# A ring of two raw weight places instead of four, earlier expert weights, first projection weights ahead of the other transfers

## The chip, the cores and the metric

The kernel runs on one core of a Trainium2 chip. The metric is device time in microseconds (us) of one execution. Three runs of the kernel before gave 681.19 us as the median (680.13 to 682.99). The profile shown here is of one execution that took 680.27 us, of which the profiler's span holds 678.3.

## The reference

One layer on 256 tokens of width 1024, in float32: a norm, one wide projection, a mixer of two branches (a sparse attention with compressed, selected and windowed keys, and a gated recurrence, HGRN2), a gated merge with two branch projections, an output projection with residual, and then a mixture of 32 experts, two per token, and a last norm. What matters for the time is cut to this:

```python
def reference(x, ...):
    h = rmsnorm(x, attn_norm)
    proj = h @ w_in                                   # 1024 x 4888
    o_nsa = nsa_mixer(...); o_hg = hgrn2_mixer(...)
    mixed = gate_nsa * (o_nsa @ w_br_nsa) + gate_hg * (o_hg @ w_br_hg)
    x = x + mixed @ w_out
    x = x + hier_moe(rmsnorm(x, ffn_norm), ...)
    return rmsnorm(x, final_norm)

def hier_moe(h, ...):
    ...
    for e in range(32):                               # w_gate, w_up 1024 x 512, w_down 512 x 1024
        hid = silu(t @ w_gate[e]) * (t @ w_up[e])
        out = out + combine[:, e:e + 1] * (hid @ w_down[e])
```

## The kernel before, in words

The work has two stages. **The front** computes everything up to the router. Its weights come as 30 blocks of 1 MB (two of them smaller) in the order of the list `FRONT`: f0, f1, q0, q1, c0, c1, b0, b1, a0, a1, i0, i1, g0, g1, m20 to m31, h0, h1, m00 to m11, n0, n1, o00, o10, o01, o11. A block is loaded into a *raw* place (`load_front`), then split into a high and a low part (`split_part`): ScalarE copies the high part in a reduced format, VectorE subtracts it from the raw block. TensorE then forms three products per pair (`three`: all high products first, L442, then high by low and low by high, L444 and L445). The split of a block is issued when the block before it begins on TensorE, and `load_front` is called behind it. A split is also held back until the third last group of products so far has ended (`HOLD`, `marks`). Attention and recurrence steps stand in the list `todo` and are put between groups of products (`fill`).

**The experts** follow in eight rounds of four (`hidden`, `prepare`, `down`): gate product, up product, down product. Their weights are 96 matrices of 2 MB, loaded by `load_expert` in the order of the list `pieces`: in the first round four gate pieces (`k`), four up, then down pieces, one of them in halves.

**Memory.** All large tiles with the tag `w2` share 11 double slots of 2 MB (16 KB of each partition): the input, the raw ring, the parts of each block (`wsp`), long-lived data of the front, and the expert pieces. A second tag `w` has three slots of 1 MB. Which slot a tile gets is decided when the program is built: one whose earlier tile is no longer needed. Nearly all transfers stand in one queue, SyncE's (SP): each is issued in order, and a transfer that waits for its place holds up all behind it. The table `EARLY` names front blocks at which expert pieces are put into that queue, so that experts' weights come while the front still computes. In each engine's own queue the order is fixed when the program is built, too, by a scheduler that works with its own estimates.

The first round's expert weights are 13 pieces. After them, the next transfer (the second round's gate weights) needs a place that the first round's gate product frees.

Of the kernel before, what the change touches and what calls it, by code (L numbers as in the profile page):

```python
# [9 lines left out]
F32 = mybir.dt.float32  # L10
# [58 lines left out]
def _level_masks():  # L69
# [4 lines left out]
    while h < 128:  # L74
# [10 lines left out]
FRONT = ["f0", "f1", "q0", "q1", "c0", "c1", "b0", "b1", "a0", "a1", "i0", "i1", "g0", "g1",  # L85
         "m20", "m21", "m30", "m31", "h0", "h1", "m00", "m01", "m10", "m11",
         "n0", "n1", "o00", "o10", "o01", "o11"]
WIDTH = {n: 2048 for n in FRONT}
WIDTH["c0"] = WIDTH["c1"] = 1120
FOFF = {}  # L90
# [82 lines left out]
CUTS = [slice(0, 256), slice(256, 512)]  # L173
LAST = [(slice(0, 2), slice(0, 1024)), (slice(2, 4), slice(0, 512)), (slice(2, 4), slice(512, 768)), (slice(2, 4), slice(768, 1024))]
GATE_V = (0, 0)
EARLY = {"a0": 1, "i1": 1, "m31": 1, "m10": 1, "n0": 1, "o00": 1, "o10": 1, "o01": 2}
HOLD = 3
FILLS = {"n0": 2, "m10": 3, "m20": 1, "m11": 3, "m01": 3, "m00": 3, "h0": 1, "h1": 1, "i": 1, "m30": 1, "g": 1}

# [2 lines left out]
def tile_block(ctx, tc, x, xp, xa, xb, wf, wcmp, vec, rows, consts, lmask, w_gate, w_up, w_down, out, dbg=None, manual=False):  # L182
    nc = tc.nc
    PE, V, S, G = nc.tensor, nc.vector, nc.scalar, nc.gpsimd
    dbg = dbg or {}

    cp = ctx.enter_context(tc.tile_pool(name="cp", bufs=1))
# [9 lines left out]
    def pair(name, dtype=F32):  # L197

        return big.tile([128, 4096], dtype, tag="w2", bufs=PAIRS, name=name)
# [17 lines left out]
    def two(t, n=1024, **k):  # L217
        return t[:, :n], t[:, n:]
# [6 lines left out]
    def load_x(name, src):  # L225
        t = slot(name)
        v = t.rearrange("p (t d) -> p t d", t=2)
        for tt in range(2):
            nc.sync.dma_start(v[:, tt], src[128 * tt:128 * tt + 128, :])
        return v  # L230

    xs = two(pair("xab"), 2048)
# [4 lines left out]
    vc_ = cp.tile([128, vec.shape[1]], F32, name="vc_")  # L237
    kept = _C["causal"][0]
    cs = cp.tile([128, kept], F32, name="cs")
    cm_ = kb2("2x", "cm_")  # L240
    lm = cp.tile([128, 8, 128], U8, name="lm")

    def row(name, t):
        o, n = ROWS[name]
        nc.sync.dma_start(t, bass.AP(tensor=rows.tensor, offset=rows.offset + o, ap=[[0, 128], [1, n]]))
        return t
# [8 lines left out]

    ident = C("ident")
    raws, his, los, marks, splits = {}, {}, {}, [], []
    ring = [h for _ in range(2) for h in two(pair("raw"), 2048)]
    to_load, to_split = list(FRONT), list(FRONT)

    def load_front():
        if to_load:
            n = to_load.pop(0)
            w = WIDTH[n]
            raws[n] = ring[FRONT.index(n) % 4][:, :w]
            step = w // 2 if n == FRONT[0] else w
            for o in range(0, w, step):
                nc.sync.dma_start(raws[n][:, o:o + step], bass.AP(tensor=wf.tensor, offset=wf.offset + FOFF[n] + 128 * o,
                                                                  ap=[[step, 128], [1, step]]))
                if n == FRONT[0] and o == 0:  # L270
                    nc.sync.dma_start(xs[1][:, :1024], xb)

    def after(i):

        return tc.issue_after(getattr(i, "ins", i))

    def split_part(n, c, behind=()):

# [74 lines left out]

    load_front()
    load_front()
    nc.sync.dma_start(vc_, vec)
    nc.sync.dma_start(cs, consts[:, :kept])
    xv = load_x("x", x)
    load_front()
    nc.sync.dma_start(cm_[:, :consts.shape[1] - kept], consts[:, kept:])  # L360
    hgn = row("hgn", cm_[:, 384:])
    brow = row("br", cp.tile([128, 36], F32, name="brow"))
    lmf = slot("lmf")[:, :1152].rearrange("p (l t) -> p l t", l=9)
    nc.sync.dma_start(lmf, lmask)


    hh_, hl_ = two(pair("hhl", F32R), 2048)
# [53 lines left out]
    def token_factors():  # L421

        prx = bank("ns", "prx")
        with after(marks[-3]):
            PE.matmul(prx[:, :256], one.to_broadcast([128, 128]), rxd, start=True, stop=True)
        V.tensor_copy(rxb, prx[:, :256])

    rt = VC("rt").rearrange("p (k e) -> p k e", k=8)
    G.memset(ones, 1.0)
# [2 lines left out]
        G.tensor_copy(before, lmf[:, 8])  # L432
        G.tensor_tensor(rt, rt, VC("fe")[:, :, None].to_broadcast([128, 8, 36]), op=OP.mult)
    wcm = slot("wcm")
    nc.sync.dma_start(wcm, wcmp)
    dump("hT", hhi.bitcast(F32))


# [578 lines left out]
    xv = load_x("x2", xp)  # L1017
# [455 lines left out]
```

## Time and profile before

| | before |
|---|---|
| median of 3 runs | 681.19 us |
| the profiled execution | 680.27 us |
| its span | 678.3 us |
| TensorE (PE) busy | 548.6 us, 81% of the span |
| VectorE (DVE), ScalarE (ACT) busy | 212.8 us, 145.4 us |
| transfers | 238.84 MB, mean 352 GB/s |
| experts' weights in the chain that ended last | 20% up, 15% gate, 16% down |

The page's slices show two stages. Up to about 240 us TensorE is busy all the time and the transfers come and go; after that the transfers run at about 427 GB/s to the end, and TensorE is busy in parts. Time that an engine idles while another is the bound costs nothing.

### The profile page before, as it was taken

The numbers are of one execution on the slowest core, as the hardware profiler recorded it, in microseconds if no ns is written. First come the engines' busy times: TensorE is split into PE (matmuls) and PEld (weight loads), VectorE is DVE, ScalarE is ACT, GpSimd is POOL, SyncE is SP. The second block draws the span as 40 slices with busy tenths as digits, with TensorE's granted clock in tenths as the row PEclk, the third lists the DMA queues.
The fourth block names the chain that finished last, engine by engine and source line by source line (L and its number), as shares of the span: only waits on it lengthen the run. The fifth ranks groups of instructions, "written<-read, shape, count | busy, mean of one in ns | idle before, by whom it ended". The sixth has DMA issues, their size and how long they took to land.

```text
span 678.3 us, 8658 instructions
## 1 busy us (share of the span) xinstructions
PE 548.6 (81%) x3692; PEld 314.8 (46%) x3692; DVE 212.8 (31%) x430; ACT 145.4 (21%) x235; POOL 32.0 (5%) x50
## 2 busy tenths in 40 slices
PE   8989999999999999987758468766846877594574
PEld 6988777888898854342114114212411421141121
DVE  5686856777558342121002102101210110020012
ACT  5433348466455310100000000000000000000003
POOL 0411500200000000000000000000000000000001
PEclk8999999999999999989679788967968796697888
DMA  8856463463578999999999999999999999999993
GB/s 343 346 190 229 143 254 119 151 230 129 191 269 320 425 421 427 427 422 431 427 428 427 426 426 426 429 425 432 423 426 431 422 429 428 426 427 429 420 389 119
DMA packets 26443, 238.84 MB, mean 352 GB/s; under 512 B 2720, under 2 KB 5280, under 8 KB 10144
## 3 DMA queue, kind: packets, MB, share of 16 engines
q1 hardware_dynamic: 26112, 237.44, 84.9%
q8 instruction: 31, 0.51, 0.3%
q10 hardware_dynamic: 288, 0.79, 0.3%
q14 instruction: 12, 0.10, 0.0%
HBM read 237.17 MB, written 1.05 MB: 351 GB/s over the span
## 4 chain that ended last, share of the span: by engine, by line
DMA 50%; PE 29%; DVE 1%; ACT 0%; issue 0%; SPq 0%; POOL 0%; POOLq 0%; DVEq 0%; ACTq 0%
DMA we<-in_w_up 20%; DMA we<-in_w_gate 15%; DMA wh<-in_w_down 10%; DMA wd<-in_w_down 6%; PE pu L1258 5%; PE pws L442 3%; PE pws L445 3%; PE pws L444 3%; PE pg L1258 2%; PE py L1315 2%; PE pga L1146 2%; PE pwo L442 1%; PE pwo L445 1%; PE pwo L444 1%; PE pno L903 1%; PE pnt L880 1%
## 5 line engine op out<-in xcount | busy, mean ns | idle before, releaser
L1258 PE MATMUL pg<-we,xe 128*32 128x512 f32 x512 | 94.3, 723 | 52.1 <-DMA we<-in_w_gate 52.1
L1258 PE MATMUL pu<-we,xe 128*32 128x512 f32 x512 | 91.2, 721 | 47.3 <-DMA we<-in_w_up 43.5
L1286 DVE SCALAR_TENSOR_TENSOR h<-pu,wv,h 128x512 f32<-128x512 f32 x8 | 8.7, 1089 | 246.2 <-PE pu L1258 246.2
L286 DVE TENSOR_TENSOR wsp<-raw,wsp 128x2048 fp32r<-128x2048 f32 (+3 forms) x34 | 68.2, 2011 | 33.7 <-ACT wsp L282 33.5
L1258 PEld LDWEIGHTS pg<-we,xe 128*32 128x32 f32 x512 | 20.1, 128 | 121.7 <-DMA we<-in_w_gate 73.4
L1258 PEld LDWEIGHTS pu<-we,xe 128*32 128x32 f32 x512 | 20.4, 129 | 113.1 <-DMA we<-in_w_up 61.9
L282 ACT ACTIVATE wsp<-raw 128x2048 fp32r<-128x2048 f32 (+3 forms) x34 | 56.3, 1663 | 45.0 <-PE pws L445 14.9
L1298 ACT ACTIVATE ys<-py,wv 128x512 fp32r<-128x512 f32 (+1 forms) x17 | 11.3, 663 | 243.2 <-PE py L1315 211.8
L1315 PE MATMUL py<-wh,hT 128*32 128x512 f32 x112 | 49.4, 594 | 3.7 <-DMA wh<-in_w_down 3.7
L1315 PE MATMUL py<-wd,hT 128*32 128x512 f32 x336 | 50.6, 595 | 0.0
L445 PE MATMUL pws<-hhl,wsp 128*128 128x256 f32 x192 | 49.3, 288 | 0.7 <-DVE wsp L286 0.7
L444 PE MATMUL pws<-hhl,wsp 128*128 128x256 f32 x192 | 49.1, 287 | 0.0
L1280 ACT ACTIVATE h<-pg,wv 128x512 f32<-128x512 f32 x8 | 9.2, 1144 | 150.6 <-PE pg L1258 150.6
L445 PEld LDWEIGHTS pws<-hhl,wsp 128*128 128x128 f32 x192 | 37.4, 195 | 1.0 <-DVE wsp L286 0.9
L444 PEld LDWEIGHTS pws<-hhl,wsp 128*128 128x128 f32 x192 | 37.4, 195 | 0.0
L442 PE MATMUL pws<-hhl,wsp 128*128 128x256 f32 x192 | 34.1, 297 | 1.3 <-ACT hhl L401 1.3
L1299 DVE SCALAR_TENSOR_TENSOR ys<-py,wv,ys 128x512 fp32r<-128x512 f32 (+1 forms) x17 | 12.2, 719 | 69.0 <-ACT ys L1298 68.4
L1146 PE MATMUL pga<-lm,x 128*128 128x128 f32 x256 | 30.3, 276 | 0.0
L444 PE MATMUL pxs<-wsp,hhl 128*128 128x512 f32 (+1 forms) x80 | 29.9, 377 | 0.2 <-DVE wsp L286 0.2
L442 PEld LDWEIGHTS pws<-hhl,wsp 128*128 128x128 f32 x192 | 27.3, 194 | 5.1 <-ACT hhl L401 2.4
L445 PE MATMUL pxs<-wsp,hhl 128*128 128x512 f32 (+1 forms) x80 | 29.5, 372 | 0.0
L1146 PEld LDWEIGHTS pga<-lm,x 128*128 128x128 f32 x256 | 29.3, 192 | 0.2 <-DVE lm L1137 0.2
(252 smaller groups left out, 684.3 us busy)
## 6 DMA issues: line engine op xcount, KB each, us to landing
we<-in_w_gate SPq DMA_DIRECT2D x32, 2048.0 KB, 34.3
we<-in_w_up SPq DMA_DIRECT2D x32, 2048.0 KB, 34.5
wd<-in_w_down SPq DMA_DIRECT2D x21, 2048.0 KB, 39.1
raw<-in_wf SPq DMA_DIRECT2D x27, 1024.0 KB, 4.8
wh<-in_w_down SPq DMA_DIRECT2D x15, 1024.0 KB, 30.0
wd<-in_w_down SPq DMA_DIRECT2D x3, 1024.0 KB, 35.6
wd<-in_w_down SPq DMA_DIRECT2D x3, 512.0 KB, 23.6
wd<-in_w_down SPq DMA_DIRECT2D x6, 256.0 KB, 8.6
```

The lines of the kernel that those rows point to most:

```text
L282: i = S.activation(his[n][:, c], raws[n][:, c], AF.Copy)
L286: splits.append((i, V.tensor_tensor(los[n][:, c], raws[n][:, c], his[n][:, c].bitcast(F32), op=OP.subtract)))
L442: PE.matmul(out_, lh, rh, start=start and i == 0, stop=False, skip_group_check=True)
L444: PE.matmul(out_, lh, rl, start=False, stop=False, skip_group_check=True)
L445: last = PE.matmul(out_, ll, rh, start=False, stop=stop and i == n - 1, skip_group_check=True)
L1146: i = PE.matmul(pgs[q, n][:, 128 * k:128 * k + 128], xv[:, tt, 512 * n + 128 * k:512 * n + 128 * k + 128], sel[q][:, tt], start=tt == 0 an ...
L1258: i = PE.matmul(p[32 * e:32 * e + 32], xes[q][:, k, 32 * e:32 * e + 32], W["k", k // 2][:, e, k % 2] if by_rows else W[4 * q + e][:, k], s ...
L1280: S.activation(h, pg.rearrange("p (c j) -> p c j", j=4), AF.Silu, scale=r)
L1286: V.scalar_tensor_tensor(h, pu.rearrange("p (c j) -> p c j", j=4), r, h, op0=OP.mult, op1=OP.mult)
L1298: return (S.activation(hi[:, c], p[:, c], AF.Copy, scale=wv), V.scalar_tensor_tensor(lo[:, c], p[:, c], wv, hi[:, c].bitcast(F32), op0=OP. ...
L1299: V.scalar_tensor_tensor(lo[:, c], p[:, c], wv, hi[:, c].bitcast(F32), op0=OP.mult, op1=OP.subtract))
L1315: PE.matmul(py[n][32 * e:32 * e + 32], hTs[q][:, j, 32 * e:32 * e + 32], WD[4 * q + e, j][:, 512 * n:512 * n + 512], start=j == 0, stop=j ...
```

## The change

- The raw ring has two places of 1 MB in one double slot (it had four in two). The first three loads become two, and a block's load waits for the split of the block two before it instead of four. One double slot more is left for parts (`wsp`) and expert pieces.
- `EARLY` puts eleven expert pieces into the queue during the front instead of nine: new ones at b0, a second at n0 and one at n1; the one at i1 is gone.
- The first half of f0 is issued ahead of the second half of the input (`xb`); vectors, constants and the input for the norm follow f1, the masks and `wcmp` follow whatever block was last issued.
- The copy of the token factors (`rxb`) is put behind the last split.

```diff
-EARLY = {"a0": 1, "i1": 1, "m31": 1, "m10": 1, "n0": 1, "o00": 1, "o10": 1, "o01": 2}
+EARLY = {"b0": 1, "a0": 1, "m31": 1, "m10": 1, "n0": 2, "n1": 1, "o00": 1, "o10": 1, "o01": 2}
...
-    ring = [h for _ in range(2) for h in two(pair("raw"), 2048)]
+    ring = two(pair("raw"), 2048)
+    last_dma = []
...
-            raws[n] = ring[FRONT.index(n) % 4][:, :w]
+            raws[n] = ring[FRONT.index(n) % 2][:, :w]
...
-                nc.sync.dma_start(raws[n][:, o:o + step], bass.AP(tensor=wf.tensor, offset=wf.offset + FOFF[n] + 128 * o,
-                                                                  ap=[[step, 128], [1, step]]))
+                i = nc.sync.dma_start(raws[n][:, o:o + step], bass.AP(tensor=wf.tensor, offset=wf.offset + FOFF[n] + 128 * o,
+                                                                      ap=[[step, 128], [1, step]]))
+                last_dma.append(i)
                 if n == FRONT[0] and o == 0:
-                    nc.sync.dma_start(xs[1][:, :1024], xb)
+                    with after(i):
+                        nc.sync.dma_start(xs[1][:, :1024], xb)
...
     load_front()
     load_front()
-    nc.sync.dma_start(vc_, vec)
-    nc.sync.dma_start(cs, consts[:, :kept])
-    xv = load_x("x", x)
-    load_front()
-    nc.sync.dma_start(cm_[:, :consts.shape[1] - kept], consts[:, kept:])
-    hgn = row("hgn", cm_[:, 384:])
-    brow = row("br", cp.tile([128, 36], F32, name="brow"))
+    with after(last_dma[-1]):
+        nc.sync.dma_start(vc_, vec)
+        nc.sync.dma_start(cs, consts[:, :kept])
+        xv = load_x("x", x)
     lmf = slot("lmf")[:, :1152].rearrange("p (l t) -> p l t", l=9)
-    nc.sync.dma_start(lmf, lmask)
+    with after(last_dma[-1]):
+        nc.sync.dma_start(cm_[:, :consts.shape[1] - kept], consts[:, kept:])
+        hgn = row("hgn", cm_[:, 384:])
+        brow = row("br", cp.tile([128, 36], F32, name="brow"))
+        nc.sync.dma_start(lmf, lmask)
...
-        V.tensor_copy(rxb, prx[:, :256])
+        with after(splits[-1][1]):
+            V.tensor_copy(rxb, prx[:, :256])
...
-    nc.sync.dma_start(wcm, wcmp)
+    with after(last_dma[-1]):
+        nc.sync.dma_start(wcm, wcmp)
```

Three places show what the built programs make of it. The first is the head of SP's queue. Before (the third row holds the two halves of f0, the next f1; the first `raw_74` is q0, the second q1):

```order
L271 DMA xab_67<-in_xb 128x1024
L268 DMA raw_73<-in_wf 128x1024 x2
L268 DMA raw_73<-in_wf 128x2048
L356 DMA vc__69<-in_vec 128x328
L357 DMA cs_70<-in_consts 128x202
L229 DMA x_81<-in_x 128x1024
L229 DMA x_81<-in_x 128x1024 [waits DMAHW0_49]
L268 DMA raw_74<-in_wf 128x2048 [waits DMAHW1_49]
L360 DMA cm__71<-in_consts 128x384 [waits DMAHW2_49]
L245 DMA cm__71<-in_rows 128x128 [waits DMAHW3_49]
L245 DMA brow_87<-in_rows 128x36 [waits DMAHW4_49]
L364 DMA lmf_89<-in_lmask 128x1152 [waits DMAHW5_49]
```

Now, from f1 on (the last two rows are q0 and q1):

```order
L273 DMA raw_73<-in_wf 128x2048
L360 DMA vc__69<-in_vec 128x328
L361 DMA cs_70<-in_consts 128x202
L229 DMA x_80<-in_x 128x1024
L229 DMA x_80<-in_x 128x1024 [waits DMAHW0_49]
L365 DMA cm__71<-in_consts 128x384 [waits DMAHW1_49]
L245 DMA cm__71<-in_rows 128x128 [waits DMAHW2_49]
L245 DMA brow_86<-in_rows 128x36 [waits DMAHW3_49]
L368 DMA lmf_83<-in_lmask 128x1152 [waits DMAHW4_49]
L273 DMA raw_73<-in_wf 128x2048 [waits DMAHW5_49,DVE_49]
L273 DMA raw_73<-in_wf 128x2048 [waits DMAHW6_49,DVE_49]
```

q0 has moved from before the constants and masks to behind them, and it now waits for VectorE's split of f0.

The second place is SP's queue at the end of the front. Before (the raw rows are o10, o01 and o11; the `we` rows the last gate piece and the four up pieces):

```order
L321 DMA we_1750<-in_w_gate 128x4x1024 [waits PE_49,Pool_49]
L268 DMA raw_74<-in_wf 128x2048 [waits DMAHW6_49,DVE_49]
L268 DMA raw_73<-in_wf 128x2048 [waits DMAHW7_49,DMAHW4_49,DVE_49]
L326 DMA we_1861<-in_w_up 128x4096 [waits PE_49]
L268 DMA raw_73<-in_wf 128x2048 [waits DMAHW0_49,DVE_49]
L326 DMA we_1996<-in_w_up 128x4096 [waits PE_49]
L229 DMA x2_1985<-in_xp 128x1024 [waits Pool_49]
L229 DMA x2_1985<-in_xp 128x1024 [waits DMAHW1_49]
L326 DMA we_2025<-in_w_up 128x4096 [waits DMAHW2_49,DVE_49,PE_49]
L326 DMA we_2059<-in_w_up 128x4096 [waits DMAHW3_49,DVE_49,PE_49]
L331 DMA wd_2061<-in_w_down 128x4096 [waits DMAHW6_49,DMAHW4_49,DVE_49]
```

Now (the raw rows are o00, o10, o01 and o11):

```order
L273 DMA raw_73<-in_wf 128x2048 [waits DMAHW7_49,DMAHW2_49,DVE_49]
L329 DMA we_1859<-in_w_up 128x4096 [waits PE_49]
L273 DMA raw_73<-in_wf 128x2048 [waits DMAHW1_49,DVE_49]
L329 DMA we_1861<-in_w_up 128x4096 [waits PE_49]
L273 DMA raw_73<-in_wf 128x2048 [waits DMAHW2_49,DVE_49]
L329 DMA we_1926<-in_w_up 128x4096 [waits PE_49]
L229 DMA x2_1987<-in_xp 128x1024 [waits DMAHW0_49,PE_49,Pool_49]
L229 DMA x2_1987<-in_xp 128x1024
L273 DMA raw_73<-in_wf 128x2048 [waits DMAHW4_49,DVE_49]
L329 DMA we_1999<-in_w_up 128x4096 [waits DMAHW3_49]
L334 DMA wd_2028<-in_w_down 128x4096 [waits PE_49]
```

The up pieces have moved ahead by a place or more, and o01 and o11 stand behind two and three of them, each behind a wait for VectorE.

The third place is ScalarE's queue at the end of the front: the high parts of o00, o10, o01, o11 (`wsp`), the merged branch (`mT`), the residual's squares (`sqs`). Before:

```order
L282 ACTIVATE wsp_1922<-raw_74 128x2048 [waits DMAHW1_49,PE_49,Activation_49]
L1019 ACT_TABLE_LOAD
L1019 ACTIVATE warm_97<-mhalf_96 128x1
L999 ACTIVATE mT_1890<-mg_1123 128x512 [waits DVE_49,Activation_49]
L999 ACTIVATE mT_1890<-mg_1123 128x512 [waits DVE_49]
L282 ACTIVATE wsp_1993<-raw_74 128x2048 [waits DMAHW3_49,PE_49]
L999 ACTIVATE mT_1953<-mg_1123 128x512 [waits DVE_49] x2
L282 ACTIVATE wsp_2022<-raw_73 128x2048 [waits DMAHW4_49,DVE_49,PE_49]
L282 ACTIVATE wsp_2056<-raw_73 128x2048 [waits DMAHW6_49,DVE_49,PE_49]
L1043 ACTIVATE sqs_2051,st_94<-x2_1985 128x512 [waits DMAHW0_49,DVE_49]
```

Now:

```order
L1025 ACT_TABLE_LOAD
L1025 ACTIVATE warm_95<-mhalf_94 128x1
L1005 ACTIVATE mT_1890<-mg_1121 128x512 [waits DVE_49,Activation_49]
L1005 ACTIVATE mT_1890<-mg_1121 128x512 [waits DVE_49]
L285 ACTIVATE wsp_1922<-raw_73 128x2048 [waits DMAHW2_49,PE_49]
L1005 ACTIVATE mT_1955<-mg_1121 128x512 [waits DVE_49] x2
L285 ACTIVATE wsp_1995<-raw_73 128x2048 [waits DMAHW4_49,PE_49]
L285 ACTIVATE wsp_2025<-raw_73 128x2048 [waits DMAHW6_49,PE_49,Activation_49]
L1049 ACTIVATE sqs_2054,st_92<-x2_1987 128x512 [waits DMAHW0_49,DVE_49]
L285 ACTIVATE wsp_2059<-raw_73 128x2048 [waits DMAHW2_49,PE_49,Activation_49]
```

Each of these splits has moved behind work that it stood ahead of: o00 and o10 behind a pair of `mT` rows, o11 behind the first square. In the built program the parts of o11 now lie in the slot that held the parts of o01; before they lay in one that a gate of the merge had left.

## Rows read from the trace of the kernel before

**Rows 1.** The page: its first line, and transfers in 40 slices.
```profile
span 678.3 us, 8658 instructions
...
DMA  8856463463578999999999999999999999999993
GB/s 343 346 190 229 143 254 119 151 230 129 191 269 320 425 421 427 427 422 431 427 428 427 426 426 426 429 425 432 423 426 431 422 429 428 426 427 429 420 389 119
```

**Rows 2.** Chain that ended last, in time: start, us, what; from 209 us.
```profile
209.59 0.47 PE pwo L442 x2
...
225.94 0.45 PE pwo L442 x2
...
227.31 0.88 PE pxt L1057 x8
...
234.56 0.81 PE prt L1067 x8
...
243.86 7.00 PE pg L1258 x64
...
260.68 29.07 DMA we<-in_w_up
```

**Rows 3.** SP's timeline: start, us, engine, line, operation; 234.8 to 246.5 us.
```profile
234.97 0.43 SPq L339 DMA_DIRECT2D wh<-in_w_down  x1
...
245.77 0.33 SPq L326 DMA_DIRECT2D we<-in_w_gate  x1
```

**Rows 4.** The tile wh's transfer issued at 234.97 us, from issue to landing.
```profile
DMA to landing us min/median/max: 15.6/15.6/15.6
```

**Rows 5.** The tile we's transfer issued at 245.77 us, from issue to landing.
```profile
DMA to landing us min/median/max: 9.7/9.7/9.7
```

**Rows 6.** The tile we's transfer issued at 209.62 us, from issue to landing.
```profile
DMA to landing us min/median/max: 7.9/7.9/7.9
```

**Rows 7.** Busy time by engine from 205 to 210 us; last: clock, DMA share, GB/s.
```profile
205.00:210.00 5.00, 5.00 (x42) 4.91 (x41) 5.00 (x7) 3.34 (x5) 0.00 (x0) 1.00 0.44 182
```

**Rows 8.** The page, transfers by line: count, KB each, us to landing.
```profile
raw<-in_wf SPq DMA_DIRECT2D x27, 1024.0 KB, 4.8
```

**Rows 9.** ScalarE's timeline, 199 to 220 us; in brackets the idle time before.
```profile
206.75 1.92 ACT L282 ACTIVATE wsp<-raw 128x2048 fp32r<-128x2048 f32 x1 [0.32 <-PE pws L445]
211.00 1.23 ACT L999 ACTIVATE mT<-mg 128x512 fp32r<-128x512 f32 x2 [2.33 <-DVE mg L997]
...
217.81 1.92 ACT L282 ACTIVATE wsp<-raw 128x2048 fp32r<-128x2048 f32 x1 [2.05 <-PE pwo L445]
```

**Rows 10.** VectorE's timeline, 200 to 222 us.
```profile
203.87 0.69 DVE L995 TENSOR_TENSOR mg<-pws,mg 128x512 f32<-128x512 f32 x1 [1.12 <-PE pws L445]
...
219.76 2.29 DVE L286 TENSOR_TENSOR wsp<-raw,wsp 128x2048 fp32r<-128x2048 f32 x1 [1.67 <-ACT wsp L282]
```

**Rows 11.** ScalarE's timeline at the start: the high part of q0.
```profile
16.76 1.92 ACT L282 ACTIVATE wsp<-raw 128x2048 fp32r<-128x2048 f32 x1 [1.34 <-DMA raw<-in_wf]
```

**Rows 12.** GpSimd's timeline at the start: the first use of the masks.
```profile
21.49 1.04 POOL L431 CAST lm<-lmf 128x1024 uint8<-128x1024 f32 x1 [3.35 <-DMA lmf<-in_lmask]
```

**Rows 13.** TensorE's timeline at the start: first instructions of product groups.
```profile
10.80 1.28 PE L442 MATMUL pws<-hhl,wsp 128*128 128x256 f32 x4
...
13.59 0.67 PE L442 MATMUL pws<-hhl,wsp 128*128 128x256 f32 x4
...
22.50 0.82 PE L442 MATMUL pws<-hhl,wsp 128*128 128x256 f32 x4
...
26.99 0.64 PE L442 MATMUL pws<-hhl,wsp 128*128 128x256 f32 x4
...
28.43 0.64 PE L442 MATMUL pws<-hhl,wsp 128*128 128x256 f32 x4
```

**Rows 14.** TensorE's waits, 26 to 60 us: line, releaser, us in total, times, longest.
```profile
PE phl L574 <- DVE hg L564: 1.4, 1, 1.4
PE pws L445 <- DVE wsp L286: 0.7, 1, 0.7
```

More of the change, by code (lines that the diff above doesn't have):

```diff
@@ L257, in tile_block, with after @@
     raws, his, los, marks, splits = {}, {}, {}, [], []
-    ring = [h for _ in range(2) for h in two(pair("raw"), 2048)]
+    ring = two(pair("raw"), 2048)
+    last_dma = []
     to_load, to_split = list(FRONT), list(FRONT)
+    def after(i):
+        return tc.issue_after(getattr(i, "ins", i))
     def load_front():
@@ L264, in load_front @@
             w = WIDTH[n]
-            raws[n] = ring[FRONT.index(n) % 4][:, :w]
+            raws[n] = ring[FRONT.index(n) % 2][:, :w]
             step = w // 2 if n == FRONT[0] else w
             for o in range(0, w, step):
-                nc.sync.dma_start(raws[n][:, o:o + step], bass.AP(tensor=wf.tensor, offset=wf.offset + FOFF[n] + 128 * o,
-                                                                  ap=[[step, 128], [1, step]]))
+                i = nc.sync.dma_start(raws[n][:, o:o + step], bass.AP(tensor=wf.tensor, offset=wf.offset + FOFF[n] + 128 * o,
+                                                                      ap=[[step, 128], [1, step]]))
+                last_dma.append(i)
                 if n == FRONT[0] and o == 0:
-                    nc.sync.dma_start(xs[1][:, :1024], xb)
-    def after(i):
-        return tc.issue_after(getattr(i, "ins", i))
+                    with after(i):
+                        nc.sync.dma_start(xs[1][:, :1024], xb)
     def split_part(n, c, behind=()):
```

## Prediction

> **What bounds the kernel now.** I read the page's slices of the transfers first [rows 1]: they run at about 427 GB/s from slice 13 (220 us) to the end, and below that in nearly every slice before. So there are two regimes, and the question is how one hands over to the other. The chain that ended last, read in order of time [rows 2], shows it: TensorE's products up to 250.86 us (the first round's gate product begins at 243.86), and from about 260 us on transfers of expert weights, the first of them a wait of 29.07 us. The front is bound by TensorE, the rest by the transfers, which never pause again. The end is therefore fixed by one event, the landing of the first transfer of the second round; all behind it follows at the same pace, whatever the change does. In SP's timeline this transfer is issued at 245.77 us [rows 3], when the gate product has freed its first place, and it lands 9.7 us later, at 255.5 [rows 5]. It lands behind the last piece of the first round, issued at 234.97 and landed 15.6 us later, at 250.6 [rows 3, 4]. So in the kernel before the queue is not yet empty when the first place comes free. 4.9 us lie between the two landings, which is 2 MB at 427 GB/s [rows 1]. A 2 MB transfer that finds the queue nearly empty takes 7.9 us from issue to landing [rows 6], 3.0 more than its own 4.9.
>
> This gives the rule for the sum. With D as the delay of TensorE at its first gate product, the first transfer of the second round is issued at 245.8 + D and lands at the later of two times: 245.8 + D + 7.9, or 4.9 after the last piece of the first round. The end shifts by as much as this landing differs from 255.5. Even with D = 0 the best is 253.7, a gain of 1.8 us: 2 MB less in the queue would save 4.9, but 3.0 to 3.1 of that are lost because the queue runs dry before a place is free.
>
> The Trainium skill, "DMA: Bandwidth & Descriptors", section "Anatomy of one DMA", gives a fixed part of about 2.0 us (measured on GpSimd's path) and 436 GB/s for the rest; by it 2 MB would take an estimated 6.8 us where the row has 7.9, and the sum below would come out 1.1 us lower. The row decides.
>
> **The change part by part.**
>
> *An expert piece more, early.* The piece at b0 goes into a stretch in which the transfers have room (107 to 254 GB/s in slices 4 and 5 [rows 1]). It costs nothing there, and takes 2 MB, 4.9 us, from the backlog. By the rule above it is worth 1.8 us at most.
>
> *The end of the front, on ScalarE and VectorE.* Here the loss lies. In the built order the split of o10 has gone behind the second pair of merged rows on ScalarE, the split of o11 behind the first square, and the parts of o11 lie in the slot of those of o01. TensorE's blocks take 5.45 us each: o00 begins at 209.59, o11 three blocks later at 225.94 [rows 2]. A high part takes 1.92 us on ScalarE [rows 9], a low part 2.29 on VectorE, an evacuation 0.69 [rows 10].
> - o00: its low part comes behind the evacuation of n1's first half and ends at about 210.6, one us into the block; the four high products that now stand first (4 x 0.23 us, from 0.45 for two [rows 2]) cover 0.9. Cost 0.1.
> - o10: its high part ran at 206.75, ahead of the second pair of `mT`, which ran at 211.00 [rows 9]. Now it follows that pair. The pair's second half needs n1's last products (209.6); VectorE takes it up when o00's low part and a merged row are done (211.2), spends two operations of 0.65 (212.5), ScalarE copies 0.6 (213.1), then o10's high part to 215.0 and its low part to 217.3. TensorE is there at 215.1, has 0.9 of high products, and waits from 216.0 to 217.4: 1.35.
> - o01: its raw block is issued when o00's low part is done, 210.6, and lands 4.8 us later [rows 8], at 215.4; parts by 219.7, needed at 221.9. Cost nothing.
> - o11: its high part ran at 217.81 [rows 9] and its low part at 219.76 [rows 10], well ahead of 225.94. Now the high part cannot begin until TensorE has left o01, at 225.94 + 1.45 = 227.4. It is done at 229.3, the low part at 231.6. Meanwhile TensorE has eight transposes (0.88 us in [rows 2]), which wait 0.3 for the residual's second add, then idles 0.8 until 229.35, does four high products, waits 0.35 for ScalarE's copies, and has the logits until the low part is there. Cost 1.45.
> Together 0.1 + 1.35 + 1.45 = 2.9 us, all on TensorE's path to the gate product. Behind the ring's waits are queued, on SP, the up pieces, the second copy of x and o11 itself: from 205 to 210 us the transfers were busy for 0.44 of the time before [rows 7]; now a gap of some 2 us comes at 211, and I count the last piece of the first round to land near 250 (14 MB from 215.4, 2.45 us each). So 4.9 after it is 255, and the first of the two times decides.
>
> *The start.* The first half of f0 ahead of `xb` lets TensorE begin up to 1.1 us earlier. But q0 pays for it: it has gone behind x, the constants, the rows and the masks. Before it landed by 16.76 [rows 11], the masks at 21.49 [rows 12]; the sum of bytes up to both is the same, so q0 now lands at about 21.4. Its high part is done at 23.35, its low part at 25.65. TensorE wants the low part after four high products: it began q0 at 22.50 and q1 at 28.43 [rows 13], so it is 2.5 us late, and what f0 won in front of this wait is gone. Of these 2.5 the stall of 0.7 in q1 goes (its low part is now in time), and 1.4 are a stall that TensorE has at the first diagonal product anyway [rows 14]: VectorE, which it waits for there, is busy with its own queue and, as I count it, gets to that point no later. 0.4 is left. Bounds: 0 (another 0.6 in such stalls is to be had further on), and 2.5 + 1.4 = 3.9 if nothing is absorbed and the first groups after the wait run at half clock (below). I take 0.4, as the stall's row stands right there.
>
> *The ring of two.* A block's load now starts when the split two blocks before it is done. One block is four groups of 1.44 us (26.99 to 28.43 [rows 13]), 5.8, and more with fills; a load takes 4.8 [rows 8] and a split 4.2. Two blocks are 11.5, so 2.5 us remain, and the splits are held back by TensorE's marks in any case. Cost 0; behind an expert piece, at 9.7 [rows 5], it would be up to 2.4 late. *The fourth slot for parts*: ScalarE's splits wait for TensorE's products of the held-back group [rows 9], as far as the row tells, not for a slot; worth 0. *The copy of the token factors* stood behind the same split before: 0.
>
> **The sum.** D = 2.9 + 0.4 = 3.3. First transfer of the second round: 245.8 + 3.3 + 7.9 = 257.0, against 255.5: the end comes 1.5 us later. The profiled execution took 680.27 us, its span 678.3 and 2.0 around it, which gives 681.8. It lay 0.9 below the median of 681.19, so the forecast is 682.7. About 0.5% (3.4 us) is what a measurement of this kernel can tell from no change; the forecast lies inside it, 681 to 684.5 as its own range.
>
> **The rivals.**
> 1. *The earlier piece pays in full.* If the waits of o10 and o11 are covered and TensorE reaches its gate product 3.1 us earlier than before, 4.9 are saved: 676.3. For it speaks that the queue is the bound from there on; against it that D would have to be -3.1, while the order of the queues gives 2.9 on the other side. Between D = -1.6 and 5.2 it ends as no change. Chance 0.08 of over 0.5%.
> 2. *The clock falls in the new waits.* TensorE begins its work at the start after an idle gap, and soon after it the groups from 10.80 take 2.8 us (to 13.59) where a later one takes 1.44 [rows 13]: the granted clock is at half, 1.2 instead of 2.4 GHz, for some 3.2 us, which costs about 1.6. If this follows the wait in q0 and the one at o11, and nothing of the first is absorbed, D is 3.3 + 3.2, the first transfer lands at 260.2, and the end is 4.7 late: 685.9. It decides from D = 5.2 on. For it: two waits of over one us in short succession. Against it: the stall of 1.4 at the first diagonal [rows 14] is followed by no such stretch. The Trainium skill, "TensorE: Matmul & The Clock Gate", section "HAM oscillation — how this bites in real kernels", says that waits for data between bursts of products throttle the clock again; this is that rival. Chance 0.22.
> 3. *The ring of two starves TensorE in mid-front.* Four expert pieces ahead of raw blocks at up to 2.4 us each: D up to 13, 689 or more. Against it: a raw load is issued ahead of each piece, and the next comes a block later. Chance 0.04.
>
> **How the numbers follow.** Forecast 0.66, rivals 0.08, 0.22 and 0.04. Faster by over 0.5%: 0.08; within 0.5%: 0.66; slower: 0.26. The range of 8 in 10 leaves out rival 1 in full and the far end of rivals 2 and 3: 678.5 to 687.
>
> **What would show it.** Right: the gate product begins 2.5 to 4.5 us later; the first transfer of the second round takes about 8 us, not 9.7; ScalarE's last raw split begins when o01's products end; q0's high part begins at 21 to 23; the diagonal's stall is gone. Wrong: a gate product no later than 243.9, a split of o11 ready when TensorE comes to it, q0 in time, or half-clock stretches before 250.

## The result, and the profile after

The changed kernel takes 687.18 us (median of 6 runs, 684.62 to 688.22), the kernel before, run beside it, 680.13 (6 runs). The ratio is 1.0098 [1.0084, 1.0112]: slower by 1.0%, more than the 0.5% that I called no change. The forecast was 682.7, 1.5 later than the kernel before; measured are 7.05, and the time lies just outside the range (687.0). Of the cases on record, rival 2 came in the main, the clock that falls in the new waits (685.9, chance 0.22), and not the likeliest.

The page's lines for the changed kernel, which answer to [rows 1]:

```profile
span 685.3 us, 8659 instructions
...
DMA  8648533363479989999999999999999999999993
GB/s 319 244 158 311 208 124 123 124 246 123 176 312 372 417 351 428 430 427 425 428 428 425 428 427 427 428 426 428 425 427 428 424 430 428 428 425 428 421 394 122
```

The two regimes are still there: about 427 GB/s from slice 15 on (257 us; counted from 0, as the prediction counts), less before. In the kernel before that began with slice 13. What has moved is the place of the handover. SP's timeline (start, us, engine, line, operation) at the issue of the last piece of the first round and of the first of the second, which answers to [rows 3]:

```profile
243.48 0.42 SPq L342 DMA_DIRECT2D wh<-in_w_down  x1
254.28 2.04 SPq L329 DMA_DIRECT2D we<-in_w_gate  x2
```

and from issue to landing of the transfer at 254.28, where [rows 5] had 9.7:

```profile
DMA to landing us min/median/max: 7.8/7.8/7.8
```

It lands at 262.07, 6.6 us later than in the kernel before. The last piece of the first round, issued at 243.48, took this long:

```profile
DMA to landing us min/median/max: 11.2/11.2/11.2
```

So it had landed at 254.67, 7.4 earlier: the first transfer of the second round finds a queue that is all but empty and takes what [rows 6] said it would. TensorE's timeline has the gate product in the changed kernel and in the kernel before at

```profile
252.29 1.06 PE L1264 MATMUL pg<-we,xe 128*32 128x512 f32 x8
...
243.79 0.64 PE L1258 MATMUL pg<-we,xe 128*32 128x512 f32 x4
```

So D is 8.5, where my sum had 3.3.

TensorE's timeline of the changed kernel where q0 begins (in brackets the idle time before and what ended it), against [rows 13]:

```profile
23.04 0.74 PE L448 MATMUL pws<-hhl,wsp 128*128 128x256 f32 x4 [2.63 <-ACT wsp L285]
...
25.37 0.58 PE L451 MATMUL pws<-hhl,wsp 128*128 128x256 f32 x1 [1.47 <-DVE wsp L289]
...
27.02 1.05 PE L448 MATMUL pws<-hhl,wsp 128*128 128x256 f32 x4
...
29.59 0.63 PE L448 MATMUL pws<-hhl,wsp 128*128 128x256 f32 x2
```

Two waits, with five products between them; behind them a group takes 2.57 us (27.02 to 29.59), where one takes 1.44 in [rows 13]. (q0's block, asked for at 11.96, had landed 9.0 us later, at 20.99.) The table by stretches says why. Its last three columns are the granted clock, the transfers' share and GB/s; first the changed kernel, then the kernel before, in the same two stretches:

```profile
24.40:31.20 6.80, 5.83 (x27) 5.83 (x28) 5.72 (x8) 3.06 (x4) 0.61 (x1) 0.50 0.52 175
...
236.00:240.00 4.00, 4.00 (x13) 3.24 (x13) 0.00 (x0) 0.00 (x0) 0.00 (x0) 0.57 0.98 408
```
```profile
24.40:31.20 6.80, 6.14 (x51) 5.94 (x51) 3.70 (x5) 3.60 (x4) 1.21 (x1) 1.00 0.82 322
236.00:240.00 4.00, 3.69 (x47) 3.51 (x48) 3.55 (x19) 1.15 (x4) 0.80 (x2) 1.00 1.00 428
```

The clock is at its lower level, 1.2 GHz, from 24.39 to 31.21 us, with 27 products where the kernel before has 51; and once more from 236.01 to 239.43. The last four blocks wait where the prediction put the waits:

```profile
214.14 0.50 PE L450 MATMUL pwo<-wsp,mT 128*128 128x512 f32 x1 [0.27 <-DVE wsp L289]
220.87 0.50 PE L450 MATMUL pwo<-wsp,mT 128*128 128x512 f32 x1 [0.98 <-DVE wsp L289]
231.96 0.66 PE L1063 MATMUL pxt<-cs,x 128*128 128x128 f32 x4 [0.34 <-DVE x L1041]
233.23 1.18 PE L448 MATMUL pwo<-wsp,mT 128*128 128x512 f32 x4 [0.61 <-ACT wsp L285]
```

The shift against the kernel before, block by block: f0 -1.5, f1 -2.4, q0 +0.5, q1 +4.75, c0 +3.8, then +3.34 to +3.38 from b0 to o00, o10 +3.9, o01 +5.2, o11 +7.5, gate product +8.5. Between c0 and b0 there are two moves: behind the first diagonal product, where TensorE waits less than before, the shift is down to +2.1, and at b0 it goes up again by 1.3. There TensorE waits for VectorE, which is late with b0's low part:

```profile
50.90 1.97 PE L606 MATMUL phl<-hg,hg 128*128 128x64 f32 x16 [1.05 <-DVE hg L623]
```

In the kernel before this wait is 0.48. b0's raw block was asked for at 37.89, when the split of c0 had freed its place in the ring of two, and took

```profile
DMA to landing us min/median/max: 6.2/6.2/6.2
```

where the same block in e2 and e4 (below) takes 4.6 and 4.7 and costs nothing. No transfer stood ahead of it in the queue. So there are three losses, 2.1 at the start, 1.3 at b0 and 5.2 at the end of the front; the second is rival 3 in small, though without the weight piece ahead of the block that rival 3 supposed.

### The profile page after: what moved, and what is told of

Read it like the earlier page. It is cut to its first block, busy times and chain, and to the rows that moved or that the text cites. A ratio compares the mean times of both kernels' runs of the same rounds, so it can differ in the third digit from the quotient of the medians.

```text
span 685.3 us, 8659 instructions
## 1 busy us (share of the span) xinstructions
PE 554.9 (81%) x3692; PEld 317.4 (46%) x3692; DVE 213.6 (31%) x430; ACT 145.3 (21%) x235; POOL 33.5 (5%) x50
## 3 DMA queue, kind: packets, MB, share of 16 engines
HBM read 237.17 MB, written 1.05 MB: 348 GB/s over the span
## 5 line engine op out<-in xcount | busy, mean ns | idle before, releaser
L285 ACT ACTIVATE wsp<-raw 128x2048 fp32r<-128x2048 f32 (+3 forms) x34 | 56.2, 1663 | 48.7 <-PE pws L451 21.4
L1321 PE MATMUL py<-wd,hT 128*32 128x512 f32 x336 | 53.6, 609 | 0.0
L1321 PE MATMUL py<-wh,hT 128*32 128x512 f32 x112 | 50.8, 608 | 3.5 <-DMA wh<-in_w_down 3.5
L451 PE MATMUL pws<-hhl,wsp 128*128 128x256 f32 x192 | 50.0, 291 | 1.5 <-DVE wsp L289 1.5
L450 PE MATMUL pws<-hhl,wsp 128*128 128x256 f32 x192 | 49.7, 289 | 0.0
L451 PEld LDWEIGHTS pws<-hhl,wsp 128*128 128x128 f32 x192 | 38.1, 198 | 1.8 <-DVE wsp L289 1.7
L450 PEld LDWEIGHTS pws<-hhl,wsp 128*128 128x128 f32 x192 | 38.1, 198 | 0.0
L448 PE MATMUL pws<-hhl,wsp 128*128 128x256 f32 x192 | 34.8, 299 | 3.9 <-ACT wsp L285 2.6
L448 PEld LDWEIGHTS pws<-hhl,wsp 128*128 128x128 f32 x192 | 27.6, 197 | 8.2 <-ACT wsp L285 3.0
```

Source lines behind the costliest of these rows:

```text
L285: i = S.activation(his[n][:, c], raws[n][:, c], AF.Copy)
L448: PE.matmul(out_, lh, rh, start=start and i == 0, stop=False, skip_group_check=True)
L450: PE.matmul(out_, lh, rl, start=False, stop=False, skip_group_check=True)
L451: last = PE.matmul(out_, ll, rh, start=False, stop=stop and i == n - 1, skip_group_check=True)
L1321: PE.matmul(py[n][32 * e:32 * e + 32], hTs[q][:, j, 32 * e:32 * e + 32], WD[4 * q + e, j][:, 512 * n:512 * n + 512], start=j == 0, stop=j ...
```

## The experiments

Twelve runs followed: eleven kernels, and the changed one again. *D* is the start of the first gate product against the 243.79 of the kernel before, *landing* that of the first gate piece of the second round, both in the profiled execution; the ratio is to the kernel before on the same chip (there its median lies between 679.5 and 680.1, so compare ratios rather than medians).

| run | D | landing | span | median | ratio |
|---|---|---|---|---|---|
| before | 0 | 255.5 | 678.3 | 680.1 | |
| changed | +8.5 | 262.1 | 685.3 | 687.2 | 1.0098 [1.0084, 1.0112] |
| e1 q0 ahead | +0.2 | 256.2 | 679.0 | 679.1 | 0.9989 [0.9977, 1.0002] |
| e2 old pieces | +2.7 | 258.6 | 681.4 | 684.5 | 1.0072 [1.0049, 1.0096] |
| e3 both | -3.3 | 252.2 | 676.3 | 677.7 | 0.9968 [0.9955, 0.9981] |
| e4 clock held | +2.9 | 257.0 | 680.7 | 683.3 | 1.0056 [1.0038, 1.0074] |
| e5 tenth piece | -3.2 | 252.2 | 675.1 | 676.7 | 0.9952 [0.9940, 0.9965] |
| e6 without n1 | -3.1 | 253.3 | 676.2 | 678.1 | 0.9979 [0.9969, 0.9988] |
| e7 pieces alone | +2.7 | 256.6 | 680.3 | 681.6 | 1.0028 [1.0017, 1.0039] |
| e8 f0 second | -1.4 | 253.9 | 678.3 | 680.0 | 0.9994 [0.9984, 1.0004] |
| e9 f0 first | -0.8 | 254.7 | 677.8 | 679.6 | 0.9991 [0.9979, 1.0002] |
| e10 e2, clock held | -0.4 | 255.6 | 678.4 | 680.6 | 1.0018 [1.0005, 1.0030] |
| e11 before, 36 warm | 0.0 | 255.4 | 678.4 | 680.1 | 1.0006 [0.9991, 1.0020] |
| e12 changed again | +9.2 | 263.0 | 687.2 | 686.1 | 1.0083 [1.0064, 1.0103] |

From the landing to the end of the span lie 422.8 to 424.4 us in all fourteen profiles: the handover does fix the end, to within 1.6 us.

**e1: q0 asked for ahead of the constants.**
```diff
-    with after(last_dma[-1]):
-        nc.sync.dma_start(cm_[:, ...], consts[:, kept:])   # rows, lmf too
     ...
     list(first)
+    with after(last_dma[-1]):
+        nc.sync.dma_start(cm_[:, ...], consts[:, kept:])   # rows, lmf too
```


> The changed kernel with one move: q0's block is asked for ahead of the constants, the two rows and the masks instead of behind them; ring of two, late pieces and all else stay. Theory A (half of the loss is q0's late landing, the half clock it leaves included; the other half is made after o00 by the moved pieces): q0 lands near 17 to 18 instead of 20.99, the stalls of 2.63 and 1.47 us at q0 and the half clock at 24.39 to 31.21 go, block b0 starts within 0.5 us of the kernel before instead of 3.4 later, the late part (+5.2 from o00 to pg) stays; pg starts 5 later than before, the first gate piece of the second round lands near 259, and the time is 683 to 684.5. Rival B (the ring of two costs it, wherever q0 is asked for): the start stays 3 us late, 686 to 688. Rival C (all of the loss is the start): time 680 to 681.

q0 lands at 16.65, begins at 19.88 and not at 23.04, and no half clock follows; b0 is 2.35 us *earlier* than in the kernel before (theory A had said within 0.5). The last four blocks lose 3.6 all the same, with the same four waits:

```profile
207.36 0.50 PE L449 MATMUL pwo<-wsp,mT 128*128 128x512 f32 x1 [0.27 <-DVE wsp L289]
214.09 0.50 PE L449 MATMUL pwo<-wsp,mT 128*128 128x512 f32 x1 [0.95 <-DVE wsp L289]
225.19 0.66 PE L1062 MATMUL pxt<-cs,x 128*128 128x128 f32 x4 [0.34 <-DVE x L1040]
226.46 1.18 PE L447 MATMUL pwo<-wsp,mT 128*128 128x512 f32 x4 [0.61 <-ACT wsp L285]
```

Both halves of theory A are seen, but its time was missed by 4 us, since the start did not only lose nothing but won 2.4 to 3.4. That the profiled execution (680.8) has rival C's time is not for rival C's reason: the late loss is there, and the start's gain covers it.

**e2: the old table of pieces.**
```diff
-EARLY = {"b0": 1, "a0": 1, "m31": 1, "m10": 1, "n0": 2, "n1": 1, "o00": 1, "o10": 1, "o01": 2}
+EARLY = {"a0": 1, "i1": 1, "m31": 1, "m10": 1, "n0": 1, "o00": 1, "o10": 1, "o01": 2}
```


> The changed kernel with the table of early weight pieces of the kernel before (nine pieces, none at b0, one at i1, one at n0, none at n1); the ring of two, the fourth slot for parts and the late q0 stay. Theory A: the start is 3.3 us late as in the changed kernel with its half clock, but from o00 to pg nothing more is lost (within 1 us); TensorE reaches pg 3 to 4 us later than before; by the landing rule (issue 245.8 plus D plus 7.9) the first gate piece of the second round lands at 257 to 258, 1.5 to 2.5 later than before: 681.5 to 683. Rival B (the late loss comes from the ring of two, not from the pieces): the late part stays, 686 to 688. Rival C (the start's 3.3 us pass to the end in full): 683.5 to 684.

D is +2.66 at o00 and +2.68 at the gate product: the late loss is gone with the pieces, ring of two or not, so rival B falls. But theory A's landing (257 to 258) and time were missed: the last first-round piece lands 3.1 late, the first gate piece 4.9 behind it, and so the start's loss passes on in full, as rival C had it. The profiled execution took 683.59 us; the median is 684.5, and the runs spread from 682.4 to 687.1.

**e3: both.** The edits of e1 and e2 together.

> Both moves at once: q0 ahead of the constants and the old table of early pieces; ring of two, fourth parts slot and f0's first half ahead of xb stay. Theory A: block starts within 0.7 us of the kernel before from q0 to pg, no half clock between 24 and 32 or at 236, first gate piece of the second round lands within 1 us of 255.5: 679 to 681.5, no difference. Rival B (the ring of two loses time of its own): 683 or more, with the loss at stalls on raw blocks between q0 and o11. Rival C (f0's head start, 1.5 us, pays): 678 or less.

Better than theory A: q0 2.6 earlier, b0 2.3, gate product 3.3 earlier, landing at 252.2, and 0.3% faster than the kernel before. Rival C had the size right (678 or less), though f0's start is not the whole cause (e9).

**e4: TensorE kept busy while q0's parts are made.**
```diff
+    pw2 = bank("ns", "pw2")
+    for _ in range(36):
+        PE.matmul(pw2[:, :256], wz[:, :128], wz, start=True, stop=True)
     for j in range(2):
         run(columns_first(f"q{j}", evac_q(j), hhi, hlo, 8))
```


> The changed kernel with 36 idle products (the 128x256 bf16 product of the program's first lines, into a bank that nobody reads) put on TensorE between the token factors and q0, so that it doesn't stand idle from 20.4 to 24.4 while q0's parts are made; q0 lands as late as in the changed kernel. If the half clock at 24.39 to 31.21 is made by the idle stretch (theory A): the granted clock stays 1.0 there, q1 starts 1.5 to 2.5 later than before instead of 4.75, b0 0.3 to 1 later instead of 3.4, and the time falls by about 2.7 to 684 to 685. Rival B (the clock falls whatever TensorE does there, or the lost time is the wait for the parts alone): b0 still 3 us late or more, time 687 as the changed kernel.

The same stretch as above, in e4:

```profile
24.40:31.20 6.80, 6.17 (x51) 5.96 (x51) 6.10 (x9) 3.53 (x4) 0.61 (x1) 1.00 0.53 177
```

and TensorE's timeline there:

```profile
20.18 4.09 PE L953 MATMUL pw<-wz 128*128 128x256 bf16 x36
24.03 0.72 PE L448 MATMUL pws<-hhl,wsp 128*128 128x256 f32 x4
...
25.50 0.38 PE L451 MATMUL pws<-hhl,wsp 128*128 128x256 f32 x1 [0.63 <-DVE wsp L289]
```

q0 begins a whole microsecond later than in the changed kernel, and yet q1 is 2.4 us earlier and b0 4.0: full clock, 51 products and not 27. This is theory A: 2.7 of the 4.0 are there ahead of b0, as it said, and the other 1.3 are the wait at b0, which e4 does not have. The time is 683.3 where the changed kernel's is 687.2, 3.9 less; the second half clock, near 236, is missing in e4 too. "HAM oscillation — how this bites in real kernels" in the Trainium skill's "TensorE: Matmul & The Clock Gate" says that waits for data between bursts of products throttle the clock; the trace of e4 agrees, since work without any use, put into the wait, keeps the clock at 1.00 where it was 0.50.

**e5: a tenth piece.** e3 with `"b0": 1` added to the old table.

> e3 (q0 ahead of the constants, old table of early pieces) with one weight piece more at b0, so ten pieces by o01, and still only one at n0 and none at n1. The DMA queue runs without a gap from o00 to the end of the first round, so a piece of 2 MB that is taken out of that stretch should let its last piece land up to 4.9 us earlier than in e3 (247.3). Then the first gate piece of the second round is bound by its issue (242.5 plus 7.9 = 250.4 instead of 252.2): theory A, 1.0 to 1.8 less than e3: 676 to 677, with no new stall before o00. Rival B: the places for the pieces, not the queue, set when the last ones are asked for, and nothing changes: 677.5 to 678. Rival C: the piece at b0 delays a raw block and TensorE waits in the b and a blocks: 679 or more.

Rival B in the mechanism: the last piece of the first round is asked for at 231.80 (e3: 231.67) and lands at 247.28 (247.29), the first gate piece at 252.18 (252.19). The piece taken out of the late stretch brings the last ones no earlier, since their places set when they are asked for. The time is still the best of all, 0.5% below the kernel before, and so within what theory A said. Its interval overlaps that of e3, and in the profiles the 1.2 us between the two spans lie behind the landing (422.9 against 424.1), where neither theory looks.

**e6: e1 without the piece at n1.** `EARLY` of e1 without `"n1": 1`.

> e1 (q0 ahead of the constants, the new table) without the new piece at n1: b0 1, a0 1, m31 1, m10 1, n0 2, o00 1, o10 1, o01 2. It tells the two new pieces of the last blocks apart. In e1 the four last blocks lose 3.5 to 3.6 us against the old table, 2.2 of it in four stalls. Theory A (each piece asked for ahead of a raw block delays it by its share of the queue, and two in a row, at n0 and n1, add up): without the one at n1 the blocks lose under 1 us, pg starts 3 or more us earlier than in e1, the first gate piece lands at 252 to 253, and the time is 677 to 678.5. Rival B (the second piece at n0 alone does it): pg as late as in e1 and 679. Rival C (the new piece at b0 costs, not the late ones): as rival B, with the loss before o00.

Theory A: no wait at o00 to o11, the four blocks lose nothing (-3.13 at o00, -3.12 at the gate product). The whole late loss of 3.6 goes with the one piece at n1; the second at n0 costs TensorE nothing, though the last first-round piece lands 1.15 later than in e3. A piece at n1 beside a single one at n0 was not tried. ScalarE's timeline shows the split of o11 and the first square, in e6 and then in e1:

```profile
218.11 1.92 ACT L285 ACTIVATE wsp<-raw 128x2048 fp32r<-128x2048 f32 x1 [3.47 <-DMA raw<-in_wf]
221.29 0.63 ACT L1048 ACTIVATE sqs<-x 128x512 f32<-128x512 f32 x1 [1.27 <-DVE x L1040]
```
```profile
222.89 0.63 ACT L1048 ACTIVATE sqs<-x 128x512 f32<-128x512 f32 x1 [8.66 <-DVE x L1040]
...
224.49 1.91 ACT L285 ACTIVATE wsp<-raw 128x2048 fp32r<-128x2048 f32 x1 [0.88 <-ACT sqs L1048]
```

Without the piece at n1 the split is back ahead of the square, and begins when its block lands.

**e7: the kernel before with the new table alone.** The first line of e2's diff, the other way round.

> The kernel before with nothing but the new table of early pieces; ring of four, three double slots for parts, old order of the first transfers. Theory A (the moved pieces cost 3.5 us of TensorE's time at the last four blocks whatever the ring, and the handover rule passes on what lies beyond 1.8): block starts as before up to o00, pg 2.5 to 3.6 later, the first gate piece lands at 256.2 to 257.5 instead of 255.5: 680.5 to 682. Rival B (the late loss needs the ring of two): pg within 0.7 us of before, 679.5 to 680.5. Rival C (the early piece at b0 pays in full, as my first rival of the prediction had it): 676 to 677.

Theory A: -0.87 at o00, +2.70 at the gate product, 3.6 lost, with a ring of four as with a ring of two. By the rule it lands at 245.8 + 2.7 + 7.9 = 256.4; it landed at 256.58.

**e8 and e9: f0's first half ahead of xb, in the kernel before.**
```diff
-                    nc.sync.dma_start(xs[1][:, :1024], xb)
+                    with after(i):
+                        nc.sync.dma_start(xs[1][:, :1024], xb)
...
+    with after(f0_last[-1]):     # e9 only; the same around cm, rows, lmf, wcm
         nc.sync.dma_start(vc_, vec)
```


> The kernel before with nothing but f0's first half asked for ahead of the second input block; ring of four, old table. In the changed kernel f0 starts 1.5 us earlier and f1 2.4, since the half clock of the kernel before at 10.24 to 13.65 doesn't come. Theory A (this head start, not the ring or the fourth slot, is what e1 and e3 gain): f0 -1.5, f1 -2.4, q0 -2.4, b0 -2 to -3.4, passed on whole to the handover: first gate piece at 252.2 to 253.5, 677 to 678.5. Rival B (the raw blocks hold q0 where it was, 22.5 to 23, whenever f0 begins): b0 within 1 us of before, 679 to 680.

> e8 again as it was meant: in e8 the small block of vectors had taken the first place on SP's queue, so f0's first half became second and not first, and landed at 6.46 instead of 5.4 to 5.6. Now all later transfers are held behind f1, as in the changed kernel, and q0 stays ahead of the constants; ring of four, old table. Theory A (the head start of f0, not the ring or the fourth parts slot, is what e1 and e3 gain): f0 starts at 6.5, no half clock near 10 to 13.5, f1 at 13.9, q0 2 or more earlier than before, pg 2.5 to 3.3 earlier, first gate piece at 252.2 to 253, time 677 to 678.5. Rival B (it needs the ring of two with its fourth parts slot, by which the raw of q0 is split earlier): q0 and b0 within 1.5 of the kernel before, 679 to 680.

e8 missed its purpose: with nothing to hold it, the vectors' block went first and f0 second. e9 has f0 1.64 and f1 2.71 earlier and no half clock near 10 us, but at c0 only 0.75 of it is left, as TensorE waits for the parts of q0 and q1; the 1.4 us at the first diagonal product stay as they were. Rival B's time came in e9, 679.6, and the same in e8, 680.0. TensorE's waits from 20 to 60 us, e9 first, then e3 (line, releaser, us in total, times, longest):

```profile
PE pws L450 <- DVE wsp L288: 1.6, 2, 1.5
PE phl L579 <- DVE hg L569: 1.4, 1, 1.4
PE phl L605 <- DVE cdav L580: 0.6, 1, 0.6
```
```profile
PE pws L450 <- DVE wsp L289: 1.6, 2, 1.5
...
PE phl L579 <- DVE hg L569: 0.3, 1, 0.3
PE phl L605 <- DVE cdav L580: 0.2, 1, 0.2
```

In e3 VectorE does the decay of the first half ahead of q1's low part, and comes to the product that the diagonal waits for at 36.17, not 38.14. This order came with the ring of two, the fourth parts slot, the later raw loads and the held copy of the token factors together; which of them makes it was not taken apart.

**e10: e2 with e4's idle products.**

> e2 (late q0, old table of pieces) with the 36 idle products of e4 ahead of q0. Theory A (all that q0's late landing costs comes by the half clock that it leaves, 3.4 to 4.0 us; the wait itself is covered by f0's head start): b0 0.4 to 0.9 earlier than in the kernel before, pg as much earlier, the first gate piece lands at 254.5 to 255.3, time 678.5 to 679.8, that is no loss against the kernel before. Rival B (the wait costs by itself, or e2's other lost time has another cause): b0 1 us or more late, 681 or more.

b0 is 0.3 earlier than in the kernel before, the gate product 0.35; in e2 both were 2.7 later. So at the start the half clock takes 3.0 of e2's loss. Against e3 the gate product is still 3.0 late: that is the wait, and in part the idle products, behind which q0 begins 0.5 later than in e2. The landing, 255.6, is that of the kernel before, the median 0.2% above it: theory A in TensorE's times, a little short of it in the total.

**e11: the kernel before with `WARM = 36`.**

> The kernel before with 36 instead of 26 warming products at the program's start, nothing else: they fill the 1.29 us in which TensorE waits for f0 (f0 at 8.19). Theory A (the half clock of the kernel before at 10.24 to 13.65 also follows from an idle stretch): it doesn't come, f1 starts at 14.8 to 15.3 instead of 16.5, q0 1 to 1.7 earlier, b0 and pg 0.9 to 1.7 earlier, and the time 678 to 679. Rival B (the waits inside f0, for its parts, are enough): the half clock stays and so does the time, 679.5 to 680. Rival C (the products run past the time at which f0 could start): f0 later, 680.5.

Neither theory. From 10.20 to 13.70 the clock was 0.51 in the kernel before and is 1.00 here, and f1 begins 0.92 earlier; but the 36 products end no later than the 26 did (the idle time before f0 is 1.44 us, against 1.29), so a gap of that size alone doesn't bring the half clock. And nothing of the 0.92 gets past c0 (0.00): TensorE waits 1.5 for q1's parts, as in e9, where [rows 14] have 0.7.

**e12: the changed kernel once more.**

> The changed kernel itself once more. In its first profile the clock is at half a second time, at 236.01 to 239.43, though e1 and e4 have the same waits ahead of that place (0.95 to 0.98, 0.34 and 0.61 us) and stay at full clock; the four last blocks there lose 5.2 us and not 3.2 to 3.6 as in e1, e4 and e7. Theory A (the second half clock is no fixed part of the changed kernel): this profile has the first one (about 24.4 to 31.2) and not the second, pg is 6.0 to 7.0 later than in the kernel before instead of 8.5, the first gate piece lands at 259.7 to 260.7, the profiled span is 683 to 684, and over all runs 685 to 687. Rival B (it belongs to it): half clock again near 236, pg 8 to 9 later, the first gate piece at 261.5 to 262.5, span 685 to 686.

Between the two, and D (9.2) above both. The half clock at 24 us is there again (23.9 to 30.7), and the four blocks lose 3.56 at full clock: the one at 236 was no fixed part. But there is another one, elsewhere. TensorE's timeline, and the clock behind it:

```profile
52.34 1.97 PE L606 MATMUL phl<-hg,hg 128*128 128x64 f32 x16 [2.54 <-DVE hg L623]
```
```profile
54.60:58.00 3.40, 3.40 (x11) 2.63 (x10) 3.40 (x4) 1.01 (x3) 0.00 (x0) 0.50 1.03 423
```

There the raw block asked for at 37.84 took 7.7 us to land, against 6.2 in the first execution; VectorE made its low part 1.5 us later, TensorE waited 2.54 and not 1.05. With the half clock behind it, the shift goes from +2.0 ahead of b0 to +5.7, 2.4 more than in the first execution. So the ring of two does have a place without slack, at b0, and it cost something in both executions. In both, the packets of b0 and of the block behind it were nearly all through by 44.5 us, and a thin rest followed (37 GB/s up to 46.5 us in the first, 33 up to 48 in the second); why is open. This execution is the slowest of its six (689.4; the fastest took 683.3).

## Why the prediction was wrong

**The rule held.** With the D that was measured, the sum's rule gives 245.8 + 8.5 + 7.9 = 262.2; it landed at 262.07. It fits e2, e3, e5, e6 and e8 to e11 by its other half, 4.9 after the last first-round piece, as in e3 (247.29, then 252.19), and e4, e7 and e12 by the first, within 0.4. In e1 alone the piece landed 2.4 us later than either half gives (issued at 245.95, landed at 256.20): from 246 to 249 us its transfers moved only 202 GB/s, though the queue was not empty. I have no reason for that.

**The step that failed is "the start ... 0.4 is left".** Its first half was right: q0 lands at 20.99 (I had 21.4), its high part is done at 22.99 (23.35), its low part at 25.3 (25.65); and the diagonal's stall did shrink, from 1.39 to 0.19. What was left out of the sum is the clock. I knew the half clock from [rows 13] and priced it in the bound (3.9) and in rival 2, but gave that 0.22, on the ground that a wait of 1.4 at the diagonal [rows 14] has none behind it. That row was the wrong neighbour: in e1 and e3 too a lone wait of 1.47 us in q1 leaves the clock alone, while two waits (2.63 and 1.47, 3.2 and 1.47 in e2) with five products between them bring it down for 6.8 us. The nearest row was the program's own start, which the prediction had in its hand. Ahead of b0 the term measured 2.08 in the profile of the changed kernel, 2.03 in e12 and 2.66 in e2, where I had 0.4; with the clock held (e4) it was -0.60.

**The end of the front, 2.9, was a little small.** The splits stand where I put them (o10's at 216.59, less the 3.34 of shift is 213.25; I had 213.1), the waits at o10 and o11 too, and e1, e4, e7 and e12 lose 3.6. In e1 that is 0.6 in o00's block, 1.3 in o10's and 1.7 from o01 to the gate product, where I had 0.1, 1.35 and 1.45: the first is the one mis-sized. I laid it to where the splits stand on ScalarE; e6 shows what puts them there: one piece, at n1. In the first profile 1.6 more came by the second half clock; e1, e4 and e12 have the same waits there without it, so what brings it on is open.

**The sum without the clock.** e4 holds the clock, and its D of 2.9, its landing at 257.0 and its 683.3 us are nearly the forecast's 3.3, 257.0 and 682.7. That is in part luck: it has -0.7 at o00 and 3.6 behind it where I had 0.4 and 2.9.

**The zeros.** *Ring of two*: e9 and e3 differ by 2.5 us of D in its favour (with the fourth slot and the order that come with them), and at b0 it costs 1.3 in the first execution of the changed kernel and 3.6 in the second, half clock included. I had counted loads of 4.8 us against blocks, and neither a load of 6.2 to 7.7 nor VectorE's order. *The early piece* (at most 1.8): e5 lands where e3 does, 0. (The 107 GB/s that the prediction reads from slices 4 and 5 is the trace of 50 to 60 us; [rows 1] have 143 and 254 there.)

**How D = 8.5 is made up**, by the runs: f0's head start -0.8 (e9), the new order at q1 and the diagonal -2.5 (e3 less e9), q0's late landing +6.0 (e2 less e3), of which 3.0 by the clock (e2 less e10) and the rest, 3.0 at most, by the wait, the piece at n1 +3.5 (e1 less e3). That is +6.2; the other 2.3 are the second half clock (1.6) and the loss at b0 (1.3), less the 0.6 by which the first profile's start was earlier than e2's. So the change held a gain of 3.3 us of D and two unneeded losses; without them it is faster than the kernel before, by 0.2% with the two moves alone undone (e6) and by 0.3 to 0.5% with the old table (e3, e5).

## What to carry to other kernels

A late block can cost more than its wait: look at what TensorE does in the microseconds around it, and where two waits come close together, add the half clock to the price before counting any of it as absorbed by a later stall. Where transfers set the end, look for the one landing at which they take over, and price each edit by what it does to that landing. When a change mixes several moves, take it apart before giving it up: here two of them, the constants ahead of q0 and one weight piece at n1, hid a gain that the others had made.

## What the runs showed of the chip

- The half clock at q0 lasted 6.8 us in all three profiles that had both waits (changed, e2, e12), and each of the other half clocks ahead of 60 us or near 236 lasted 3.4.
- A 2 MB transfer into an empty or nearly empty queue landed 7.8 to 8.1 us after its issue (changed, e7, e12), and at the handover one waiting in line landed 4.9 behind the one ahead of it (eight profiles and the kernel before). Now and then one was slower: b0's 1 MB block took 6.2 and 7.7 in the two executions of the changed kernel, 4.6 to 5.0 in the seven other kernels with a ring of two.
- A gain ahead of a wait need not arrive: f1 came 2.7 us earlier in e9 and 0.9 in e11, and 0.75 and 0.00 of it were left at c0.
- Executions of the changed kernel lie between 684.6 and 688.2 us in one set of six and between 683.3 and 689.4 in the other; two profiles of it show half clocks at different places behind the first.
